# Sixty-four V gathers moved into the dense stage, eight expert groups per addition, and another DRAM order of the gate matrix

## The chip, the core and the metric

One NeuronCore of one Trainium2 chip runs the whole program in one launch. The metric is the device time in microseconds (us). A chip run lists the times of several executions, and their median counts. One further execution was recorded by the hardware profiler, and all rows below are of that one. Engines: PE does matmuls, DVE elementwise work, ACT activations and copies, POOL issues the indirect gathers, SP issues nearly all other DMAs.

## The reference, cut to what matters

A streaming-encoder layer (modulated norm, three mixers, output projection) is followed by a PEER expert layer. Each of 1024 tokens picks 16 experts in each of 8 heads out of 16384; expert e has a row `u_tab[e]` and a row `v_tab[e]` of 1024 float32.

```python
q = (ht @ w_q).reshape(ntok, 8, 2, 128)
s = einsum('thpd,pkd->thpk', q, sub_keys)            # two sets of 128 key scores
...                                                  # top 16 of the sums of both sets
gates = softmax(best)
act = gelu(einsum('td,thkd->thk', hb, u_tab[eb]))
out = einsum('thk,thkd->td', gb * act, v_tab[eb])
x = x + gt2 * out                                    # then a final RMS norm
```

## The kernel before

The 1024 tokens are eight tiles of 128. `front` computes the mixers for two tiles at a time (`("F", 0)` to `("F", 3)` in `PLAN`), and `product_keys` finds the experts of both. After that the expert layer is computed in two ways.

**Gathered tiles** (0, 1, 6, 7): a slot is one of a token's 128 experts. `u_slot` (L929) lets POOL gather one row of `u_tab` per token, 128 x 1024 float32, 512 KB, into a buffer `row`, and DVE multiplies it with the token and sums (L938). When all 128 slots of a tile are done, `v_slot` (L945) gathers rows of `v_tab` (L948), and DVE adds each, scaled, to `fin` (L953). Slots share 4 row buffers, 5 from the dense stage on (`RB`), so POOL runs at most that far ahead of DVE. `v_end` finishes a tile.

**Dense tiles** (2 to 5, 512 tokens): `gates` (L782) writes for each of these tokens a 128 x 128 matrix of gates, made by one-hot comparisons (DVE L793, ACT L797), a matmul (PE `gk`) and a copy to the tile `stg` (ACT L800, one buffer). A full `stg`, 16 tokens and 1 MB, goes to the DRAM tensor `gd` (L801); there are 32 of these writes. `dense` (L803) then walks all experts in 128 groups of 128: it loads the rows of U (`un`, L833), transposes them on PE (`T`, L851), splits them into a high part `uh` (ACT L852) and a low part `ul` (DVE L853), multiplies with the tokens (24 matmuls `A`), applies gelu (ACT `ag` L861), multiplies with the gates `gt` (DVE L868), splits into `w` (ACT L870, DVE L871) and multiplies with V rows (`vn`, split into `vh` and `vl`; 48 matmuls `V` per group). The V part is done for four groups at a time (`SG`), by quarters of the 1024 columns; each result is added to `acc` in SBUF (DVE L899). A gate tile `gt` holds eight groups, 2 MB (L836).

**Order.** Engines work in order; a scheduler has set each engine's order before the run. `PLAN` gives the order in the program, and a phase `("P", tu, tv)` of slots stands 3000 places lower in priority than where it is written (`PRI`), so slots fill what the front leaves. The slots of tile 0's V and tile 1's U stand beside fronts 2 and 3 and the gates; `("D",)` is the dense stage, and the slots written behind it run beside it.

Of the kernel before, what the change touches and what calls it, by code (L numbers as in the profile page):

```python
# [20 lines left out]
DM = 1024  # L21
# [9 lines left out]
AGB = 3  # L31
# [17 lines left out]
SG = 4  # L49
WB = 5  # L50
NQ = 4
UHB = 3
# [18 lines left out]
NS = HP * TOPK  # L71
NK = 128
# [15 lines left out]
def trunk(ctx, tc, x, c, w_mod, b_mod, g_mix, w_in, hgrn_lb_logits, s5_a_re, s5_a_im, s5_b_re, s5_b_im,  # L88
# [190 lines left out]
    gd = tc.dram_tile([ND // GT, 128, NK, GT], F32, name="gd")  # L279
# [505 lines left out]
    def gates(j, tT):  # L785

        for c in range(128 // GT):
# [13 lines left out]
            D.dma_start(out=gd[j * (128 // GT) + c], in_=stg)  # L801

    def dense():  # L803
# [13 lines left out]
        dpt, dpa, dpv = [pool(n, b, space=bass.MemoryType.PSUM) for n, b in (("dpt", 2), ("dpa", 2), ("dpv", 4))]  # L817
# [12 lines left out]
        for g in range(NK):  # L830
            rs_ = slice(g * 128, g * 128 + 128)
            un = dp.tile([128, DM], F32, name="un", bufs=UB)
# [10 lines left out]
            us = []  # L843
            for half in range(2):
                uh = dp.tile([128, 4, 128], F32R, name="uh", bufs=UHB)
                ul = dp.tile([128, 4, 128], F32R, name="ul", bufs=UHB)
                us.append((uh, ul))
                bk = dpt.tile([128, 4, 128], F32, name="T")
                for k in range(4):
                    kk = 4 * half + k  # L850
                    P_.transpose(bk[:, k], un[:, kk * 128:kk * 128 + 128], ident)  # L851
                S.copy(uh, bk)  # L852
                V.tensor_tensor(ul, bk, uh.bitcast(F32), OP.subtract)  # L853
            pA = dpa.tile([128, 512], F32, name="A")[:, 0:ND]
# [17 lines left out]
            ws.append(w)  # L872
            if len(ws) < SG:
                continue
            g0 = g + 1 - SG
            for qd in range(NQ):
                qs = slice(qd * QW, qd * QW + QW)
                vn = dv.tile([128, SG, QW], F32, name="vn", bufs=UB)
# [5 lines left out]
                for j0 in range(0, nt, 2):  # L884
# [440 lines left out]
```

## Time and profile before

| what | value |
|---|---|
| median of 3 runs | 3177.55 us (3175.67 to 3185.34) |
| the profiled execution, its own time | 3178.26 us |
| its span | 3176.5 us, 1.8 us less than its time |
| PE, DVE, POOL, ACT busy | 89%, 84%, 42%, 33% of the span |
| DMA moved | 896.72 MB, of it 536.94 MB by gathers |
| first and last matmul of the dense stage | 1582.1 and 3163.3 us |
| last gather issued | 3043.0 us |

The span has two halves. Up to 1582 us the fronts, the routing, the gate matrices and the slots of tiles 0 and 1 share the engines. From there to the end PE works through the 128 groups while DVE and POOL go through the slots of the other tiles. Busy shares are means over both.

### The profile page before, as it was taken

The numbers are of one execution on the slowest core, as the hardware profiler recorded it, in microseconds if no ns is written. First come the engines' busy times: TensorE is split into PE (matmuls) and PEld (weight loads), VectorE is DVE, ScalarE is ACT, GpSimd is POOL, SyncE is SP. The second block draws the span as 40 slices with busy tenths as digits, with TensorE's granted clock in tenths as the row PEclk, the third lists the DMA queues.
The fourth block names the chain that finished last, engine by engine and source line by source line (L and its number), as shares of the span: only waits on it lengthen the run. The fifth ranks groups of instructions, "written<-read, shape, count | busy, mean of one in ns | idle before, by whom it ended". The sixth has DMA issues, their size and how long they took to land.

```text
span 3176.5 us, 45427 instructions
## 1 busy us (share of the span) xinstructions
PE 2826.5 (89%) x16525; PEld 2416.8 (76%) x16525; DVE 2660.2 (84%) x5538; ACT 1037.4 (33%) x1958; POOL 1318.9 (42%) x1147
## 2 busy tenths in 40 slices
PE   5998975788788995689599999999999999999998
PEld 3765865466675874558589888899988888988887
DVE  6241798679987999889989989998999999898976
ACT  3212330132166660366622222222222222222223
POOL 0000156534444345542045545555555555354520
PEclk8998995889778995689599999999999999999999
DMA  4453587899779986898389999999999999899961
GB/s 152 117 167 122 163 308 240 306 330 317 229 239 334 312 307 234 269 346 289 133 309 346 354 327 340 349 345 340 355 334 352 346 347 345 311 326 317 352 224 60
DMA packets 419008, 896.72 MB, mean 282 GB/s; under 512 B 29416, under 2 KB 234848, under 8 KB 414688
## 3 DMA queue, kind: packets, MB, share of 16 engines
q0 software_dynamic: 147456, 536.94, 47.7%
q1 hardware_dynamic: 263680, 342.92, 32.3%
q10 hardware_dynamic: 7648, 13.96, 1.3%
q8 instruction: 130, 2.13, 0.3%
q14 instruction: 94, 0.77, 0.1%
HBM read 847.57 MB, written 46.14 MB: 281 GB/s over the span
## 4 chain that ended last, share of the span: by engine, by line
PE 43%; DVE 23%; DMA 13%; issue 11%; POOL 6%; ACT 4%; ACTq 0%; SPq 0%; POOLq 0%; DVEq 0%
PE V L139 13%; PE A L139 12%; PE bank L139 6%; DVE row L938 5%; DMA row<-in_peer_u_dram,eid 4%; DMA row<-in_peer_v_dram,eid 4%; PE wq L139 4%; POOL row L932 4%; PE bank L363 3%; DVE fin L953 3%; POOL row L948 3%; DVE oh L793 2%; PE T L851 2%; PE gk L139 1%; DMA gd<-stg 1%
## 5 line engine op out<-in xcount | busy, mean ns | idle before, releaser
L948 POOL DMA_INDIRECT row<-in_peer_v_dram,eid x512 | 636.0, 1242 | 662.5 <-DVE fin L953 365.9
L932 POOL DMA_INDIRECT row<-in_peer_u_dram,eid x512 | 643.7, 1257 | 619.3 <-DVE row L938 297.1
L139 PE MATMUL V<-vh,w 128*128 128x256 f32 x4096 | 767.7, 283 | 10.7 <-ACT w L870 4.4
L938 DVE SCALAR_TENSOR_TENSOR row<-row,h 128x1024 f32<-128x1024 f32 x512 | 619.9, 1219 | 84.7 <-DMA row<-in_peer_u_dram,eid 84.1
L953 DVE SCALAR_TENSOR_TENSOR fin<-row,wgt,fin 128x1024 f32<-128x1024 f32 x508 | 649.6, 1279 | 36.3 <-DMA row<-in_peer_v_dram,eid 33.9
L139 PEld LDWEIGHTS V<-vh,w 128*128 128x128 f32 x4096 | 643.2, 189 | 21.8 <-ACT w L870 6.9
L139 PE MATMUL V<-vl,w 128*128 128x256 f32 x2048 | 561.0, 281 | 2.6 <-DVE vl L883 2.6
L139 PE MATMUL A<-hh,ul 128*128 128x512 f32 x1024 | 406.7, 397 | 13.1 <-DVE ul L853 12.7
L139 PE MATMUL A<-hh,uh 128*128 128x512 f32 x1024 | 414.5, 405 | 0.4 <-ACT uh L852 0.3
L139 PE MATMUL A<-hl,uh 128*128 128x512 f32 x1024 | 403.5, 394 | 0.0
L139 PEld LDWEIGHTS V<-vl,w 128*128 128x128 f32 x2048 | 387.3, 189 | 7.8 <-DVE vl L883 4.5
L881 ACT CAST vh<-vn 128x1024 fp32r<-128x1024 f32 x128 | 134.7, 1052 | 460.0 <-PE V L139 427.0
L363 PE MATMUL bank<-hT,w 128*128 128x256 f32 x1152 | 269.8, 393 | 10.4 <-DMA w<-in_w_in_dram 6.9
L363 PEld LDWEIGHTS bank<-hT,w 128*128 128x128 f32 x1152 | 223.7, 198 | 45.1 <-DMA w<-in_w_in_dram 6.8
L139 PE MATMUL wq<-hT,w 128*128 128x256 f32 x1024 | 242.0, 389 | 7.4 <-DMA w<-in_peer_w_q_dram 6.0
L139 PEld LDWEIGHTS A<-hh,ul 128*128 128x128 f32 x1024 | 194.0, 189 | 53.8 <-DVE ul L853 19.9
L852 ACT CAST uh<-T 128x512 fp32r<-128x512 f32 x256 | 147.4, 587 | 264.5 <-PE T L851 261.2
L139 PEld LDWEIGHTS wq<-hT,w 128*128 128x128 f32 x1024 | 194.4, 196 | 35.1 <-DMA w<-in_peer_w_q_dram 4.7
L139 PEld LDWEIGHTS A<-hl,uh 128*128 128x128 f32 x1024 | 193.5, 189 | 36.1
L139 PEld LDWEIGHTS A<-hh,uh 128*128 128x128 f32 x1024 | 194.1, 190 | 34.7 <-ACT uh L852 1.3
L139 PE MATMUL gk<-oh 128*128 128x128 f32 x1024 | 173.6, 325 | 51.4 <-ACT oh L797 44.7
L139 PEld LDWEIGHTS gk<-oh 128*128 128x128 f32 x1024 | 160.5, 230 | 69.0 <-ACT oh L797 54.2
(423 smaller groups left out, 3977.5 us busy)
## 6 DMA issues: line engine op xcount, KB each, us to landing
vn<-in_peer_v_dram SPq DMA_DIRECT2D x128, 512.0 KB
un<-in_peer_u_dram SPq DMA_DIRECT2D x128, 512.0 KB
w<-in_w_in_dram SPq DMA_DIRECT2D x88, 512.0 KB
w<-in_peer_w_q_dram SPq DMA_DIRECT2D x64, 512.0 KB
gd<-stg SPq DMA_DIRECT2D x32, 1024.0 KB
gt<-gd SPq DMA_DIRECT2D x16, 2048.0 KB
w<-in_w_mod_dram SPq DMA_DIRECT2D x48, 512.0 KB
w<-in_w_out_dram SPq DMA_DIRECT2D x32, 512.0 KB
```

Source lines behind the costliest of these rows:

```text
L139: P_.matmul(o, l, r, start=st, stop=sp)
L363: P_.matmul(bk[:, i], w[:, k, i * 128:i * 128 + 128], hT[:, k0 + k], start=k0 + i + k == 0, stop=k0 + k == KT - 1, skip_group_check=True)
L793: V.tensor_tensor(oh, iof.unsqueeze(1).unsqueeze(1).to_broadcast([128, 2, 4, 128]), tT[:, 0:2, t4].unsqueeze(3).to_broadcast([128, 2, 4, 1 ...
L851: P_.transpose(bk[:, k], un[:, kk * 128:kk * 128 + 128], ident)
L852: S.copy(uh, bk)
L881: S.copy(vh, vn)
L932: G.indirect_dma_start(out=ur, out_offset=None, in_=u_tab, in_offset=bass.IndirectOffsetOnAxis(ap=o.eid[:, k:k + 1], axis=0))
L938: V.scalar_tensor_tensor(ur, ur, 1.0, o.h2, op0=OP.mult, op1=OP.mult, accum_out=o.act[:, k:k + 1])
L948: G.indirect_dma_start(out=vr, out_offset=None, in_=v_tab, in_offset=bass.IndirectOffsetOnAxis(ap=o.eid[:, k:k + 1], axis=0))
L953: V.scalar_tensor_tensor(o.fin, vr, o.wgt[:, k:k + 1], o.fin, op0=OP.mult, op1=OP.add)
```

## The change

- Tile 0's V slots 0 to 63 stay; slots 64 to 127 stand behind `("D",)` in `PLAN`, ahead of tile 1's V. One more buffer each of `eid` and `gate` keeps tile 0's data alive (`EB`).
- `SG` is 8: eight groups are summed in PSUM before one addition of 128 x 1024 to `acc`. V rows still come four groups at a time (`SB4`). `WB` is 8, so that one batch of `w` fills all its buffers.
- `T` is one PSUM buffer of 128 x 1024 where it was two of 128 x 512; `ul` is made by one DVE instruction per group; matmuls with `ul` come after the 16 with `uh`. `un` and `ag` have two buffers where they had three, `uh` and `ul` two of the whole width where they had three of half of it.
- `gd` lies in the order in which `gt` is read: a gate load reads 16 KB at one stretch per partition where it read runs of 512 bytes; a gate write writes 16 runs of 512 bytes per partition, 2 MB apart, where it wrote 8 KB at one stretch.
- The residual is added to `acc` four groups ahead of the end, in eight instructions.

```diff
-AGB = 3
+AGB = 2
...
-SG = 4
-WB = 5
+SG = 8
+SB4 = 4
+WB = 8
...
-UHB = 3
+UHB = 2
...
-PAD = 320
+PAD = 0
...
-EB = 3
-PLAN = [("F", 0), ("P", 0, None), ("F", 1), ("F", 2), ("G", 4), ("P", None, 0), ("P", 1, None), ("F", 3), ("D",), ("R",), ("P", None, 1), ("P", 6, None), ("P", 7, 6), ("P", None, 7), ("E",)]
+EB = 4
...
+PLAN = [("F", 0), ("P", 0, None), ("F", 1), ("F", 2), ("G", 4), ("P", None, 0, 0, 64), ("P", 1, None), ("F", 3), ("D",), ("R",), ("P", None, 0, 64, NS), ("P", None, 1), ("P", 6, None), ("P", 7, 6), ("P", None, 7), ("E",)]
...
-    gd = tc.dram_tile([ND // GT, 128, NK, GT], F32, name="gd")
+    gd = tc.dram_tile([NK // GA, 128, ND // GT, GA, GT], F32, name="gd")
...
-            D.dma_start(out=gd[j * (128 // GT) + c], in_=stg)
+            D.dma_start(out=gd[:, :, j * (128 // GT) + c].rearrange("o p a t -> p o a t"),
+                        in_=stg.rearrange("p (o a) t -> p o a t", a=GA))
...
-        dpt, dpa, dpv = [pool(n, b, space=bass.MemoryType.PSUM) for n, b in (("dpt", 2), ("dpa", 2), ("dpv", 4))]
+        dpt, dpa, dpv = [pool(n, b, space=bass.MemoryType.PSUM) for n, b in (("dpt", 1), ("dpa", 2), ("dpv", 2))]
...
-                D.dma_start(out=gt, in_=gd[:, :, g:g + GA].rearrange("c p a t -> p c a t"))
+                D.dma_start(out=gt, in_=gd[g // GA])
...
+            bk = dpt.tile([128, KT, 128], F32, name="T")
+            for k in range(KT):
+                P_.transpose(bk[:, k], un[:, k * 128:k * 128 + 128], ident)
             for half in range(2):
...
+                S.copy(uh[:, 4 * half:4 * half + 4], bk[:, 4 * half:4 * half + 4])
+            V.tensor_tensor(ul, bk, uh.bitcast(F32), OP.subtract)
             pA = dpa.tile([128, 512], F32, name="A")[:, 0:ND]
             for k in range(KT):
...
+                mm(pA, uh[:, k], hh[:, k], k == 0, False)
+                mm(pA, uh[:, k], hl[:, k], False, False)
+            for k in range(KT):
+                mm(pA, ul[:, k], hh[:, k], False, k == KT - 1)
...
+                pv = dpv.tile([128, nt, QW], F32, name="V")
+                for e0 in range(0, SG, SB4):
...
+                if g + 1 < NK:
+                    V.tensor_tensor(a, a, pv, OP.add)
+                    continue
...
-    def phase(tu, tv):
+    def phase(tu, tv, k0=0, k1=NS):
```

The built orders show it at three places. Names are the kernel's tiles; the changed kernel's line numbers are its own (its L938 and L954 are the gathers of U and V that were L932 and L948).

POOL, at the last routing of tiles 4 and 5 (the `cidx` copies), before and now:

```order
L932 DMA row<-in_peer_u_dram,eid 128x1024 x7
L716 COPY cid_6192<-cidx 128x4x8
L716 COPY cid_6192<-cidx 128x4x4
L716 COPY cid_6192<-cidx 128x4x2 x2
L716 COPY cid_6192<-cidx 128x4
L716 COPY cid_6192<-cidx 128x4x3
L932 DMA row<-in_peer_u_dram,eid 128x1024 x86
L948 DMA row<-in_peer_v_dram,eid 128x1024 x6
```

```order
L938 DMA row<-in_peer_u_dram,eid 128x1024 x7
L717 COPY cid_6192<-cidx 128x4x8
L717 COPY cid_6192<-cidx 128x4x4
L717 COPY cid_6192<-cidx 128x4x2 x2
L717 COPY cid_6192<-cidx 128x4
L717 COPY cid_6192<-cidx 128x4x3
L938 DMA row<-in_peer_u_dram,eid 128x1024 x4
L954 DMA row<-in_peer_v_dram,eid 128x1024 x7
L717 COPY cid_9626<-cidx 128x4x8
```

Of tile 1's U gathers 86 stood behind this routing, now 4; 63 V gathers of tile 0 that stood ahead of tile 1's U stand behind front 3. DVE's order follows: where the gates of the first two dense tiles are done, 276 slots have been consumed before and 285 now; up to the first `ul` of the dense stage 386 before and 323 now.

PE, in the dense stage between two groups, before and now:

```order
L851 MATMUL T<-ident,un 128x128 x4
L139 MATMUL V<-vh,w 128x256
L139 MATMUL V<-vl,w 128x256
L139 MATMUL V<-vh,w 128x256
L139 MATMUL V<-vl,w 128x256
L139 MATMUL V<-vh,w 128x256
L139 MATMUL A<-hh,ul 128x512
L139 MATMUL A<-hl,uh 128x512
L139 MATMUL A<-hh,uh 128x512
```

```order
L898 MATMUL V<-vh,w 128x256
L140 MATMUL A<-hh,ul 128x512 x8
L849 MATMUL T<-ident,un 128x128 x8
L898 MATMUL V<-vh,w 128x256
L898 MATMUL V<-vl,w 128x256
L140 MATMUL A<-hh,uh 128x512
L140 MATMUL A<-hl,uh 128x512
```

Before, V matmuls or matmuls of the other half of `T` stand between a transpose and what needs it all through the stage. Now each batch of eight groups begins with four that have at most two V matmuls behind their eight transposes (16 batches), then come groups with 8 to 26 V matmuls in between, then some 280 V matmuls almost without a break. Behind the last `A` 168 V matmuls stand before, 295 now.

DVE, around the last `w` of the dense stage, before and now:

```order
L871 TENSOR_TENSOR w<-ag,w 128x512
L868 TENSOR_TENSOR ag<-ag,gt 128x512
L871 TENSOR_TENSOR w<-ag,w 128x512
L898 TENSOR_TENSOR V<-V,gt_4569 128x512
L899 TENSOR_TENSOR acc<-acc,V 128x2x256
L898 TENSOR_TENSOR V<-V,gt_4569 128x512
L899 TENSOR_TENSOR acc<-acc,V 128x2x256
L883 TENSOR_TENSOR vl<-vn,vh 128x1024
```

```order
L867 TENSOR_TENSOR ag<-ag,gt 128x512
L959 SCALAR_TENSOR_TENSOR fin<-row,wgt,fin 128x1024
L870 TENSOR_TENSOR w<-ag,w 128x512
L959 SCALAR_TENSOR_TENSOR fin<-row,wgt,fin 128x1024
L891 TENSOR_TENSOR vl<-vn,vh 128x1024
L959 SCALAR_TENSOR_TENSOR fin<-row,wgt,fin 128x1024 x2
L909 TENSOR_TENSOR V<-V,gt_4569 128x512
L959 SCALAR_TENSOR_TENSOR fin<-row,wgt,fin 128x1024
L891 TENSOR_TENSOR vl<-vn,vh 128x1024
L910 TENSOR_TENSOR acc<-acc,V 128x2x256
L959 SCALAR_TENSOR_TENSOR fin<-row,wgt,fin 128x1024
```

Before, the last slot stands ahead of the last eight groups. Now slots go on to the end: 28 of the 1024 stand behind the last `w`. In both, some 44 slots stand among eight groups in the rest of the stage.

## Rows read from the trace of the kernel before

**Rows 1.** Busy time by stretch (windows): us, engines (instructions), granted clock, DMA.

```profile
core 0: us, PE busy (x) PEld busy (x) DVE busy (x) ACT busy (x) POOL busy (x), PEclk, DMA share, GB/s
640.00:1190.00 550.00, 477.17 (x2458) 394.72 (x2457) 494.42 (x1335) 263.64 (x579) 225.37 (x211) 0.89 0.86 295
1190.00:1335.00 145.00, 81.84 (x432) 73.66 (x430) 134.50 (x331) 18.35 (x26) 80.59 (x74) 0.64 0.76 253
1335.00:1577.00 242.00, 194.25 (x975) 162.58 (x975) 224.70 (x694) 173.71 (x409) 68.83 (x71) 0.82 0.71 256
1640.00:3040.00 1400.00, 1376.21 (x9088) 1242.50 (x9087) 1289.01 (x1711) 379.35 (x573) 765.09 (x615) 1.00 0.96 339
3045.00:3123.00 78.00, 76.96 (x538) 70.66 (x537) 52.80 (x87) 22.14 (x33) 0.00 (x0) 1.00 0.45 152
2400.00:2480.00 80.00, 80.00 (x554) 73.44 (x553) 75.01 (x102) 21.49 (x32) 45.61 (x37) 1.00 0.99 346
```

**Rows 2.** Groups by line, DVE, 640 to 1582 us.

```profile
L938 DVE SCALAR_TENSOR_TENSOR row<-row,h 128x1024 f32<-128x1024 f32 x149 | 179.7, 1216 | 25.2 <-DMA row<-in_peer_u_dram,eid 25.1
L953 DVE SCALAR_TENSOR_TENSOR fin<-row,wgt,fin 128x1024 f32<-128x1024 f32 x128 | 163.2, 1275 | 11.6 <-DMA row<-in_peer_v_dram,eid 11.2
```

**Rows 3.** Groups by line, DVE: first 1190 to 1335 us, then 1335 to 1577.

```profile
L938 DVE SCALAR_TENSOR_TENSOR row<-row,h 128x1024 f32<-128x1024 f32 x60 | 72.2, 1218 | 10.5 <-DMA row<-in_peer_u_dram,eid 10.3
L938 DVE SCALAR_TENSOR_TENSOR row<-row,h 128x1024 f32<-128x1024 f32 x44 | 53.2, 1218 | 8.1 <-DMA row<-in_peer_u_dram,eid 8.1
```

**Rows 4.** Groups by line, ACT, 1335 to 1577 us.

```profile
L797 ACT ACTIVATE oh<-oh,tT 128x128 f32<-128x128 f32 x256 | 81.2, 393 | 32.1 <-DVE oh L793 31.9
L800 ACT COPY stg<-gk 128x512 f32<-128x512 f32 x64 | 64.1, 1046 | 20.9 <-PE gk L139 12.1 <-DMA gd<-stg 8.6
```

**Rows 5.** Timeline, end of the front: SP, then PE.

```profile
1573.86 0.32 SPq L801 DMA_DIRECT2D gd<-stg  x1
1582.11 1.94 PE L851 MATMUL T<-ident,un 128*128 128x128 f32 x8 [9.37 <-issue]
```

**Rows 6.** Windows: one gate write (8 KB runs), one gate load (512-byte runs).

```profile
1553.50:1556.10 2.60, 2.33 (x13) 2.14 (x12) 2.60 (x16) 1.44 (x5) 0.00 (x0) 0.70 0.91 381
1580.50:1589.60 9.10, 7.49 (x23) 5.78 (x24) 5.64 (x8) 2.46 (x3) 0.00 (x0) 0.55 1.16 320
```

**Rows 7.** Groups by line, DVE, 1582 to 3170 us.

```profile
L853 DVE TENSOR_TENSOR ul<-T,uh 128x512 fp32r<-128x512 f32 x256 | 173.3, 685 | 21.0 <-ACT uh L852 20.8
L899 DVE TENSOR_TENSOR acc<-acc,V 128x512 f32<-128x512 f32 x248 | 167.8, 683 | 26.3 <-PE V L139 25.4
```

**Rows 8.** Timeline of SP over eight groups of experts.

```profile
2160.04 0.37 SPq L836 DMA_DIRECT2D gt<-gd  x1
2256.18 0.43 SPq L836 DMA_DIRECT2D gt<-gd  x1
```

**Rows 9.** Timeline of PE: second group of experts, nothing else to do.

```profile
1591.63 0.39 PE L139 MATMUL A<-hl,uh 128*128 128x512 f32 x1
1591.86 1.03 PE L851 MATMUL T<-ident,un 128*128 128x128 f32 x8
1593.19 0.50 PE L139 MATMUL A<-hh,uh 128*128 128x512 f32 x1 [0.29 <-ACT uh L852]
```

**Rows 10.** Waits of PE, 1582 to 3170 us: total, times, longest.

```profile
PE A L139 <- DVE ul L853: 12.7, 18, 1.7
```

**Rows 11.** Timeline of the end: DVE (three rows), and PE's last matmul.

```profile
3052.63 1.28 DVE L953 SCALAR_TENSOR_TENSOR fin<-row,wgt,fin 128x1024 f32<-128x1024 f32 x1 [0.67 <-DMA row<-in_peer_v_dram,eid]
3066.20 1.28 DVE L966 SCALAR_TENSOR_TENSOR fin<-fin,nw,row 128x1024 f32<-128x1024 f32 x1
3145.62 0.69 DVE L871 TENSOR_TENSOR w<-ag,w 128x512 fp32r<-128x512 f32 x1 [0.68 <-ACT w L870]
3163.33 0.28 PE L139 MATMUL V<-vh,w 128*128 128x256 f32 x1
```

More of the change, by code (lines that the diff above doesn't have):

```diff
@@ L831, in dense @@
             rs_ = slice(g * 128, g * 128 + 128)
[L832 removed]
+            un = dp.tile([128, DM], F32, name="un", bufs=2)
             D.dma_start(out=un, in_=u_tab[rs_])
@@ L872, in dense @@
             ws.append(w)
+            if g + 4 == NK:
+                for j in range(nt):
+                    V.tensor_tensor(acc[:, j], acc[:, j], bcast["gt2"], OP.mult)
+                    V.tensor_tensor(acc[:, j], acc[:, j], xq[:, j], OP.add)
             if len(ws) < SG:
@@ new lines, in dense @@
+                pv = dpv.tile([128, nt, QW], F32, name="V")
+                for e0 in range(0, SG, SB4):
+                    vn = dv.tile([128, SB4, QW], F32, name="vn", bufs=UB)
+                    r0 = (g0 + e0) * 128
+                    D.dma_start(out=vn, in_=v_tab[r0:r0 + SB4 * 128, qs].rearrange("(e p) d -> p e d", p=128))
+                    vh = dv.tile([128, SB4, QW], F32R, name="vh")
+                    S.copy(vh, vn)
+                    vl = dv.tile([128, SB4, QW], F32R, name="vl")
+                    V.tensor_tensor(vl, vn, vh.bitcast(F32), OP.subtract)
+                    for j in range(nt):
+                        js = slice(j * 128, j * 128 + 128)
+                        for e in range(SB4):
+                            w = ws[e0 + e]
+                            first, last = e0 + e == 0, e0 + e == SG - 1
+                            for i, (l, r) in enumerate(((w[:, 0, js], vh), (w[:, 1, js], vh), (w[:, 0, js], vl))):
+                                P_.matmul(pv[:, j], l, r[:, e], start=first and i == 0 and j % 2 == 0, stop=last and i == 2,
+                                          skip_group_check=True)
@@ new lines, in dense @@
+                a = acc[:, :, qs]
+                if g0 == 0:
+                    V.tensor_copy(a, pv)
+                    continue
+                if g + 1 < NK:
+                    V.tensor_tensor(a, a, pv, OP.add)
+                    continue
+                for j0 in range(0, nt, 2):
+                    a, p2 = acc[:, j0:j0 + 2, qs], pv[:, j0:j0 + 2]
+                    V.tensor_tensor(p2, p2, bcast["gt2"][:, qs].unsqueeze(1).to_broadcast([128, 2, QW]), OP.mult)
+                    V.tensor_tensor(a, a, p2, OP.add)
+                    for j in range(j0, j0 + 2):
+                        jk = dp.tile([128, ND], F32, name="ag", bufs=AGB)[:, 0:QW]
+                        S.activation(jk, acc[:, j, qs], AF.Square, accum_out=ss[:, j, qd:qd + 1])
+                    V.tensor_tensor(a, a, gfin[:, qs].unsqueeze(1).to_broadcast([128, 2, QW]), OP.mult)
@@ L940, in v_start @@
     def v_start(o):
-        o.wgt = pk_.tile([128, NS], F32, name="wgt")
+        o.wgt = pk_.tile([128, NS], F32, name="wgt", bufs=1)
         S.activation(o.wgt, o.act, AF.Gelu_apprx_tanh)
@@ L1010, in slots @@
             v = toks[tv]
-            v_start(v)
-        for k in range(NS):
+            if k0 == 0:
+                v_start(v)
+        for k in range(k0, k1):
             if o is not None:
@@ L1016, in slots @@
                 v_slot(v, k)
-        if v is not None:
+        if v is not None and k1 == NS:
             v_end(v)
```

53 lines of the change are left out of this document (6 added, 47 removed).

## The prediction, before the change was run

> **What bounds the kernel now.** I read the stretches first [rows 1]. From 1640 to 3040 us, the dense stage proper, PE is busy in 1376 of 1400 us at granted clock 1.00, the 2.4 GHz level, DVE in 1289 and DMA at a share of 0.96 with 339 GB/s: three resources run close to full at once. In the densest slice, 2400 to 2480, PE starts 554 matmuls in 80 us. A group has 80, so 92.4 us is about the least for eight groups, and SP's gate loads stand 96.1 us apart over eight groups [rows 8]. So PE is the bound, with some 4 us in 96 lost to what it waits for; DVE and DMA have little to give.
>
> Ahead of that, from 640 to 1577 us, DVE is the busiest: 494 of 550, 134.5 of 145 and 224.7 of 242 us [rows 1], and 343 of these 854 us are slots [rows 2]. PE waits there and its clock falls to 0.64 in the second stretch. The dense stage begins when the last gate write has left `stg`, whose memory it reuses: the write is issued at 1573.86 and the first transpose starts at 1582.11 [rows 5].
>
> I sum against the profiled execution, 3178.3 us, 1.8 over its span and 0.7 over the median of the runs. About 0.3%, some 10 us, is what a measurement can tell from no change.
>
> **The front.** By DVE's order 63 slots leave it, and what is left is shifted.
>
> *Up to 1190 us* nine more slots come in: 9 x 1.28 us [rows 2] is +12, and less if DVE's 56 idle us take some.
>
> *1190 to 1335 us.* The trace has 60 slots here [rows 3]; in the new order 38 stand from the end of the second tile's gates on, nearly all here. 22 x 1.22 is 27 us off a DVE that is busy in 134.5 of 145. I take -25, and keep -10 as an end, because the front's own chain from DVE to PE and back stays.
>
> *1335 to 1577 us.* The 44 slots here, 53 us [rows 3], go. DVE would fall from 225 to 171 us, and ACT, with 174 of 242 [rows 1], is the next bound: 145 of it are scalings and copies for 16 gate writes [rows 4], and `stg` has one buffer, so the first copy after a write waits until that has landed. Now that wait is 8.6 us in all [rows 4]. If each of 16 writes costs 2.6 us [rows 6], or 3.5 with short runs, and nothing covers it, ACT's 174 become 230, which leaves a gain of 12; if all is covered, the gain is 53. I take the middle, -32.
>
> Front: +12 - 25 - 32 = **-45**, with ends -80 and -10.
>
> **Gate matrix.** A gate write of 1 MB in long runs went at 381 GB/s with a DMA share of 0.91; a 2 MB gate load in 512-byte runs, other loads among it, at 320 GB/s with 1.16 [rows 6]. By rate the short runs cost 19% more DMA time, by rate per share 52%. For 33.6 MB that is 17 to 46 us; I take 30, off the dense stage and onto the front, where DMA is at 0.71 to 0.86 and can take it.
>
> The Trainium skill ("DMA: Bandwidth & Descriptors", Specifications) puts the least size for line rate at 512 bytes, so the layout would move nothing either way. The two windows do not agree, though others' packets are in them. By that rule the 30 us below would not come off, and the sum would be 3156.
>
> **The dense stage.**
>
> *DMA.* 63 gathers of 0.524 MB are 33 MB, 97 us at 339 GB/s. From 3045 to 3123 us the queues ran at 152 GB/s [rows 1]; up to 339 there is room for 43 us of it. With 30 from the gate loads, 24 us are left over: transfers would end near 3147 on the old clock, ahead of PE's 3163 [rows 11]. They fit, with nothing to spare.
>
> *DVE.* Slots add 63 x 1.28 = 81 us. Additions to `acc` took 248 x 0.683 = 168 and `ul` 173 us [rows 7]. An instruction twice as wide is not in the trace; its bounds are 1.22 us, that of the slot's multiply of 1024 elements from SBUF [rows 3], and 1.37, twice the 512. So 56 wide additions and 8 narrow ones make 74 to 82, 128 `ul` 156 to 175: 84 to 111 us less. DVE is not fuller than before, and per eight groups it has some 6 us less. I credit a third of PE's lost 3.7 us per eight groups to that: -20 in 16 batches (0 to -59).
>
> *PE.* The same matmuls stand in another order. Four groups in each batch have hardly anything between `T` and the `A` that needs it. The trace has one such place: 1.33 us from the first transpose to the next `A`, PE idle for 0.29 [rows 9]; the eight transposes need some 0.5 (92.4 / 8 less 24 at 0.23 and 48 at 0.115), so up to 0.8 is empty, and two V matmuls fill 0.23. Between 0.3 and 0.6 I take 0.4: 64 x 0.4 = +26. In turn PE's waits for `ul`, 12.7 us [rows 10], go, since 16 matmuls of 0.23 us now stand ahead of it: -13.
>
> *The end.* 127 more V matmuls stand behind the last `A`, so the last `w` is 15 us earlier for PE. Behind it stand 28 slots. With five row buffers 23 are still to come, 23 x 1.55 us at 339 GB/s, with six V loads 45 us. Then the last tile's finish: 14.9 us from the last slot's start to the end of the scaling [rows 11], and about 2 for the store. That is 62 behind the last `w`, where it was 31 (3145.6 to 3176.5): +31 - 15 = +16. I expect the last store to be tile 7's and no longer a dense tile's.
>
> Dense: -20 + 26 - 13 + 16 = **+9**, with ends -20 and +40. The sum is 3178.3 - 45 + 9 = **3142 us**; its own range, by the ends, is 3078 to 3208.
>
> **Rivals.**
>
> *The runs of four groups starve PE* (slower). With one `T` buffer, the next transposes wait until DVE has made `ul`; DVE works in order, and a slot ahead of `ul` can wait for its row, as slots now do for 37 us from 640 to 1582 us [rows 2]. Then `A` waits for `ul`, and nothing of V stands there to fill in. Against it: 3.7 us of matmuls stand ahead. From 0.55 us more per group of the 64 (35 us) the whole gain is gone; at 1.5 us the time is 3142 + 96 = 3238.
>
> *Gate writes hold ACT* (no change or slower). If each of the last 16 writes lands 3 us later than I allow, ACT stops in the copy behind it and DVE, PE and the dense stage's start with it: 16 x 3 = 48, 3190 us. For it: one buffer, and writes in the stretch that has just lost its other bound.
> The Trainium skill (same page, Latency and other measured facts) has copies at 164 GB/s with a 2 MiB row pitch where 512 KiB has 207; here the 16 runs of a partition lie 2 MB apart. No run here shows it yet.
>
> *All of it is gained* (faster). The front loses its 82 us, because the gates spread over it, and the lighter DVE brings PE near its floor in the dense stage: 3142 - 35 - 37 = 3070.
>
> That the slots do not move is excluded by the order; that they move and nothing shortens is the second rival.
>
> **Chances.** The forecast 0.53, starved PE 0.20, gate writes 0.12, all gained 0.15. Of the forecast's own range nine tenths lie below 3168. Faster by over 0.3%: 0.48 + 0.15 = 0.63. Within: 0.04 + 0.08 = 0.12. Slower: 0.25. The range leaves out most of the starved case and the far end of the best one: 3080 to 3205.
>
> **What would show it.** Right: the first dense transpose 30 to 60 us earlier, no slots between the third dense tile's gates, ACT's wait for gate writes up from 8.6 us in the last stretch; gate loads shorter; eight groups in 94 to 97 us; PE idle for 0.3 to 0.5 us ahead of `A` behind a bare `T`; the last store from tile 7. Wrong: a front that ends within 10 us of 1582, PE waits for `ul` of over 50 us, or eight groups in over 99 us.

## The result, and the profile after

The changed kernel took 3219.36 us in the median (3211.95 to 3226.33), the kernel before, run beside it, 3181.45: a ratio of 1.0119, 95% interval 1.0087 to 1.0151. I forecast 3142 in a range that ended at 3205. The profiled execution took 3226.33 us with a span of 3224.6. All sums below are of spans: 3224.6 - 3176.5 = +48. The medians differ by 38; the profiled execution of the changed kernel was the slowest of its four, so that some 7 us of the +48 are its own.

I cut each span in three: up to the first dense transpose (front), from there to the last `w` (dense), and what lies behind (end).

| kernel | front | dense | end | span |
|---|---|---|---|---|
| before | 1582.1 | 1563.5 | 30.9 | 3176.5 |
| changed | 1563.0 | 1583.0 | 78.7 | 3224.6 |
| difference | -19 | +19.5 | +48 | +48 |
| forecast | -45 | -22 | +31 | -36 |

(The forecast's dense stage is -20 + 26 - 13 and the 15 by which the last `w` comes earlier.)

The changed kernel's stretches, columns as in [rows 1]:

```profile
core 0: us, PE busy (x) PEld busy (x) DVE busy (x) ACT busy (x) POOL busy (x), PEclk, DMA share, GB/s
640.00:1190.00 550.00, 462.54 (x2342) 384.62 (x2340) 487.14 (x1366) 257.18 (x569) 236.59 (x218) 0.89 0.90 300
1190.00:1335.00 145.00, 101.92 (x576) 87.41 (x577) 124.50 (x319) 33.52 (x63) 53.08 (x50) 0.70 0.55 175
1335.00:1560.00 225.00, 183.98 (x956) 155.33 (x954) 156.83 (x566) 156.60 (x376) 4.65 (x24) 0.85 0.51 155
1640.00:3040.00 1400.00, 1359.03 (x8936) 1223.85 (x8935) 1212.94 (x1438) 367.75 (x566) 812.89 (x610) 1.00 0.94 338
3146.00:3211.00 65.00, 34.52 (x278) 34.15 (x278) 55.49 (x62) 15.59 (x41) 29.36 (x25) 0.78 0.82 281
```

The slots have left the stretches from 1190 to 1560 us: DMA's share there is 0.55 and 0.51, where it was 0.76 and 0.71 [rows 1], and DVE is busy in 157 of the last 225 us. Neither DVE nor ACT (157 of 225) is full there now, and yet the last 16 gate writes take 220 us from first to last, where they took 224. ACT by line, 1335 to 1560 us, answers to [rows 4]:

```profile
L798 ACT ACTIVATE oh<-oh,tT 128x128 f32<-128x128 f32 x232 | 74.1, 396 | 19.8 <-DVE oh L794 19.7
L801 ACT COPY stg<-gk 128x512 f32<-128x512 f32 x60 | 59.3, 1040 | 41.3 <-DMA gd<-stg 20.9 <-PE gk L140 20.4
```

The copy into `stg` waits 20.9 us for gate writes, where it waited 8.6. The gate loads did get shorter, as forecast: the last packet of one ends 10.0 us behind its issue in the mean over the dense stage, where it was 19.4.

Timeline of PE: the first dense transpose, which answers to [rows 5], and a place with a bare `T`, which answers to [rows 9].

```profile
1562.97 1.94 PE L849 MATMUL T<-ident,un 128*128 128x128 f32 x8 [10.58 <-DMA un<-in_peer_u_dram]
...
2178.71 1.77 PE L140 MATMUL A<-hh,ul 128*128 128x512 f32 x7
2180.32 1.03 PE L849 MATMUL T<-ident,un 128*128 128x128 f32 x8
2182.03 0.50 PE L140 MATMUL A<-hh,uh 128*128 128x512 f32 x1 [0.68 <-ACT uh L851]
```

From the transposes' start to the next `A` it is 1.71 us; eight transposes need 0.5 by the prediction's count. PE's waits from 1563 to 3170 us (total, times, longest):

```profile
PE A L140 <- ACT uh L851: 30.5, 58, 1.0
PE A L140 <- DVE ul L852: 2.1, 2, 1.2
```

The wait for `ul` has gone (12.7 us in [rows 10]); one for `uh` has come. DVE by line, 1563 to 3140 us, answers to [rows 7]:

```profile
L852 DVE TENSOR_TENSOR ul<-T,uh 128x1024 fp32r<-128x1024 f32 x128 | 156.1, 1220 | 15.5 <-ACT uh L851 15.2
L905 DVE TENSOR_TENSOR acc<-acc,V 128x1024 f32<-128x1024 f32 x56 | 68.2, 1218 | 32.5 <-PE V L898 32.3
```

An instruction twice as wide took 1.22 us, the lower of my two bounds. Timeline of DVE, the end:

```profile
3145.94 0.68 DVE L870 TENSOR_TENSOR w<-ag,w 128x512 fp32r<-128x512 f32 x1
...
3211.04 1.28 DVE L959 SCALAR_TENSOR_TENSOR fin<-row,wgt,fin 128x1024 f32<-128x1024 f32 x1 [1.23 <-DMA row<-in_peer_v_dram,eid]
3212.36 1.22 DVE L963 TENSOR_TENSOR fin<-fin,gt 128x1024 f32<-128x1024 f32 x1
...
3219.70 1.28 DVE L972 SCALAR_TENSOR_TENSOR fin<-fin,nw,row 128x1024 f32<-128x1024 f32 x1
```

The last `w` is where it was [rows 11]. 65 us later the last slot is computed, and tile 7's finish follows.

### The profile page after: what moved, and what is told of

Same layout as the page of the kernel before. It is cut to its first block, busy times and chain, and to the rows that moved or that the text cites. A ratio compares the mean times of both kernels' runs of the same rounds, so it can differ in the third digit from the quotient of the medians.

```text
span 3224.6 us, 45205 instructions
## 1 busy us (share of the span) xinstructions
PE 2831.6 (88%) x16525; PEld 2420.1 (75%) x16525; DVE 2585.1 (80%) x5214; ACT 1026.5 (32%) x1956; POOL 1375.2 (43%) x1147
## 4 chain that ended last, share of the span: by engine, by line
PE 47%; DMA 16%; DVE 15%; issue 11%; POOL 6%; ACT 5%; ACTq 0%; POOLq 0%; SPq 0%; DVEq 0%
PE V L898 13%; PE A L140 12%; PE bank L140 7%; DMA row<-in_peer_v_dram,eid 6%; PE wq L140 5%; PE bank L364 5%; POOL row L954 4%; DMA gd<-stg 3%; DVE row L944 3%; PE gk L140 3%; DMA row<-in_peer_u_dram,eid 3%; DVE fin L959 2%; POOL row L938 2%; PE T L849 2%; DMA w<-in_w_in_dram 1%
## 5 line engine op out<-in xcount | busy, mean ns | idle before, releaser
L938 POOL DMA_INDIRECT row<-in_peer_u_dram,eid x512 | 661.8, 1293 | 626.1 <-DVE row L944 294.4
L954 POOL DMA_INDIRECT row<-in_peer_v_dram,eid x512 | 677.2, 1323 | 578.6 <-DVE fin L959 288.7
L898 PE MATMUL V<-vh,w 128*128 128x256 f32 x4096 | 748.6, 282 | 18.9 <-ACT vh L889 6.1
L898 PEld LDWEIGHTS V<-vh,w 128*128 128x128 f32 x4096 | 634.4, 190 | 32.5 <-ACT vh L889 9.2
L898 PE MATMUL V<-vl,w 128*128 128x256 f32 x2048 | 569.9, 280 | 0.6 <-DVE vl L891 0.6
L140 PE MATMUL A<-hh,uh 128*128 128x512 f32 x1024 | 411.1, 401 | 32.9 <-ACT uh L851 30.5
L364 PE MATMUL bank<-hT,w 128*128 128x256 f32 x1152 | 269.9, 392 | 13.0 <-DMA w<-in_w_in_dram 10.6
L860 ACT ACTIVATE ag<-A 128x512 f32<-128x512 f32 x128 | 76.6, 598 | 621.6 <-PE A L140 602.4
L140 PE MATMUL A<-hh,ul 128*128 128x512 f32 x1024 | 258.4, 394 | 2.2 <-DVE ul L852 2.1
L364 PEld LDWEIGHTS bank<-hT,w 128*128 128x128 f32 x1152 | 222.6, 197 | 47.9 <-DMA w<-in_w_in_dram 9.5
L794 DVE TENSOR_TENSOR oh<-iof,tT 128x1024 f32<-128x1024 f32 x128 | 154.6, 1215 | 83.4 <-PE gk L140 69.0
L140 PEld LDWEIGHTS A<-hh,ul 128*128 128x128 f32 x1024 | 186.0, 189 | 38.9 <-DVE ul L852 3.2
```

The costliest lines, as they stand in the source:

```text
L140: P_.matmul(o, l, r, start=st, stop=sp)
L364: P_.matmul(bk[:, i], w[:, k, i * 128:i * 128 + 128], hT[:, k0 + k], start=k0 + i + k == 0, stop=k0 + k == KT - 1, skip_group_check=True)
L794: V.tensor_tensor(oh, iof.unsqueeze(1).unsqueeze(1).to_broadcast([128, 2, 4, 128]), tT[:, 0:2, t4].unsqueeze(3).to_broadcast([128, 2, 4, 1 ...
L898: P_.matmul(pv[:, j], l, r[:, e], start=first and i == 0 and j % 2 == 0, stop=last and i == 2, skip_group_check=True)
L938: G.indirect_dma_start(out=ur, out_offset=None, in_=u_tab, in_offset=bass.IndirectOffsetOnAxis(ap=o.eid[:, k:k + 1], axis=0))
L954: G.indirect_dma_start(out=vr, out_offset=None, in_=v_tab, in_offset=bass.IndirectOffsetOnAxis(ap=o.eid[:, k:k + 1], axis=0))
```

## The experiments

The table has the three parts of each run's span. "New order" is the new order of `gd`, "moved" the number of V slots moved, and SG the number of groups per addition. The changed kernel's front was run in three kernels, and ended at 1563.0, 1559.3 and 1550.5 us: some 6 us either way is scatter of one profile. The dense stages of e4_layout_only and e7_pitch, which differ in unused rows of DRAM alone, lie 6.5 us apart.

| run | new order | moved | SG | front | dense | end | ratio to before (95%) |
|---|---|---|---|---|---|---|---|
| e1_no_move | yes | 0 | 8 | 1603.7 | 1565.1 | 48.0 | 1.0107 (1.0072 to 1.0142) |
| e3_move_only | no | 64 | 4 | 1537.4 | 1573.3 | 100.0 | 1.0111 (1.0069 to 1.0153) |
| e4_layout_only | yes | 0 | 4 | 1600.0 | 1577.3 | 30.8 | 1.0101 (1.0052 to 1.0150) |
| e6_split96 | yes | 32 | 8 | 1587.6 | 1569.7 | 46.5 | 1.0100 (1.007 to 1.013) |
| e2_old_layout | no | 64 | 8 | 1524.0 | 1603.9 | 80.3 | 1.0128 (1.0097 to 1.0159) |
| e7_pitch | yes, padded | 0 | 4 | 1602.7 | 1583.8 | 31.6 | 1.0115 (1.0087 to 1.0142) |
| e11_load4k | yes, 4 KB loads | 0 | 4 | 1605.1 | 1555.5 | 30.6 | 1.0075 (1.0046 to 1.0104) |
| e10_move32 | no | 32 | 4 | 1577.3 | 1562.5 | 33.8 | 1.0006 (0.9988 to 1.0025) |
| e13_load_alone | loads only | 0 | 4 | 1586.5 | 1555.9 | 30.5 | 0.9969 (0.9950 to 0.9988) |
| e9_stg2 | no | 0 | 4 | 1816.7 | 1571.1 | 31.9 | 1.0766 (1.0719 to 1.0814) |
| e12_stg2_layout4k | yes, 4 KB loads | 0 | 4 | 1830.1 | 1562.9 | 30.6 | 1.0781 (1.0734 to 1.0829) |
| e14_after_load4k | yes, 4 KB loads | 64 | 8 | 1559.3 | 1583.7 | 75.2 | 1.0100 (1.0076 to 1.0124) |
| e15_drop28 | yes | 64 | 8 | 1550.5 | 1585.0 | 47.9 | 1.0015 (0.9998 to 1.0033) |
| e17_hybrid | half, 4 KB loads | 0 | 4 | 1591.2 | 1552.4 | 30.5 | 0.9996 (0.9981 to 1.0012) |
| e16_hybrid_move32 | half, 4 KB loads | 32 | 4 | 1580.4 | 1557.2 | 32.6 | 0.9997 (0.9983 to 1.0012) |

By spans, the change can be built up in three steps: the new order of `gd` alone costs 32 us (e4_layout_only), the eight-group form on top of it 9 (e1_no_move), and the move on top of both 8 (the changed kernel). But the parts do not simply add: the move alone costs 34 us (e3_move_only), and the change without the new order still costs 32 (e2_old_layout).

### The parts one by one

The changed kernel without the move (it keeps `SG = 8` and the new order):

```diff
-PLAN = [..., ("P", None, 0, 0, 64), ("P", 1, None), ("F", 3), ("D",), ("R",), ("P", None, 0, 64, NS), ...]
+PLAN = [..., ("P", None, 0), ("P", 1, None), ("F", 3), ("D",), ("R",), ...]
```

> The changed kernel with all 128 V slots of tile 0 back ahead of the dense stage; everything else as changed. Theory M (the move costs more than it gives, because the 28 slots behind the last w share DVE with the last batch's epilogue): no slot stands behind the last w, so the end comes some 45 to 50 us behind the last w where the changed kernel has 79; the front ends near 1582 us again (19 later than the changed one); total 3185 to 3195, under the changed kernel's 3219. Rival T (the new order of A, T and V in the dense stage makes all of the loss): eight groups still take 100 us, the total stays at 3205 to 3220. Rival L (gate writes in 512-byte runs hold the front): first dense transpose 10 or more us behind 1582.

The end is 48.0 us without one slot behind the last `w`, as theory M has it, but the span is 3216.8, where only the rivals T and L had it: the move is not most of the loss. The front ends at 1603.7 us, so the move brings it 41 us forward (to 1563.0), and what kept the changed front from -45 was something else. In return the move lengthens the dense stage by 18 us (1565.1 to 1583.0) and the end by 31: the moved slots do not fit.

The kernel before with the move alone:

```diff
-EB = 3
+EB = 4
-PLAN = [..., ("P", None, 0), ...]
+PLAN = [..., ("P", None, 0, 0, 64), ..., ("D",), ("R",), ("P", None, 0, 64, NS), ...]
```

> The kernel before with the move alone (64 V slots of tile 0 behind the dense stage's start, one more eid and gate buffer, one wgt buffer): old dense stage, old gate layout. In its order 42 slots stand behind the last w. Theory M: the front gains about the 19 us that it gained in the changed kernel, the end comes 80 to 100 us behind the last w, total 3210 to 3230. Rival L: without the short-run gate writes the front gains 30 us or more, first dense transpose before 1552. Rival T: total at or under 3180, since the dense stage is the old one.

Its first dense transpose, in PE's timeline:

```profile
1537.42 1.94 PE L852 MATMUL T<-ident,un 128*128 128x128 f32 x8 [8.81 <-DMA un<-in_peer_u_dram]
```

That is 44.7 us before 1582.1 [rows 5], the -45 of the forecast, and rival L's sign; the end (100.0) and the span (3210.8) are theory M's. For 42 slots stand behind the last `w`; DVE by line from 3111 us:

```profile
L954 DVE SCALAR_TENSOR_TENSOR fin<-row,wgt,fin 128x1024 f32<-128x1024 f32 x42 | 53.8, 1282 | 15.6 <-DMA row<-in_peer_v_dram,eid 14.8
```

They take 54 us, and DVE is idle for 15.6 more ahead of them. The end grows by 69 us and the dense stage by 10, more than the front gave.

The kernel before with the new order of `gd` alone (the write is the change's too):

```diff
-    gd = tc.dram_tile([ND // GT, 128, NK, GT], F32, name="gd")
+    gd = tc.dram_tile([NK // GA, 128, ND // GT, GA, GT], F32, name="gd")
-                D.dma_start(out=gt, in_=gd[:, :, g:g + GA].rearrange("c p a t -> p c a t"))
+                D.dma_start(out=gt, in_=gd[g // GA])
```

> The kernel before with the gate matrix's new order in DRAM alone. Theories M and T: within 10 us of before (3171 to 3191), first dense transpose 0 to 8 us later, DMA share in the dense stage a little lower (0.94 to 0.95 against 0.96). Rival L: ACT's wait for gate writes doubles from 27 us and the total is over 3191.

The front is 18 us later and the dense stage 14 us longer, though slots and matmuls stand in nearly the same order. ACT's waits for gate writes over the whole span, first before, then here:

```profile
ACT stg L800 <- DMA gd<-stg: 27.1, 16, 4.2
```

```profile
ACT stg L800 <- DMA gd<-stg: 64.6, 21, 6.1
```

The new order alone costs 1%, and rival L held. In this form it gives the dense stage nothing.

The changed kernel with 32 slots moved instead of 64:

```diff
-("P", None, 0, 0, 64) ... ("P", None, 0, 64, NS)
+("P", None, 0, 0, 96) ... ("P", None, 0, 96, NS)
```

> The changed kernel with the split at slot 96 in place of 64: 32 slots move, and in its order none stands behind the last w. Theory M: the end is 45 to 50 us behind the last w as without the move, the front ends 5 to 12 us earlier than 1582, total 3175 to 3192, the best of the changed family. Rival T: 3200 or more, since eight groups still take 100 us.

No slot stands behind the last `w`, and the end is 46.5. But the front gives 16 us of the 41, and the span is 3203.8, as rival T had it.

The changed kernel with the old order of `gd` (the reverse of the edit to `gd` above):

```diff
-    gd = tc.dram_tile([NK // GA, 128, ND // GT, GA, GT], F32, name="gd")
+    gd = tc.dram_tile([ND // GT, 128, NK, GT], F32, name="gd")
```

> The change with the gate matrix in the old order; all else as changed. Theory (the layout costs on the front and gives the dense stage nothing): first dense transpose at 1537 to 1548 us as in the run with the move alone (changed kernel: 1563), eight groups in 99.2 to 100 us (changed: 100.2), the part behind the last w 75 to 85 us as in the changed kernel, span 3195 to 3205. Rival (the layout pays in the dense stage when eight groups are summed, since DMA is fuller there): first transpose the same 1540, but eight groups over 100.5 and the span 3220 or more.

The front came even earlier, 1524.0. But the dense stage took 1603.9 us, 102.0 for eight groups and in three of its batches 109 to 112: the rival's number for eight groups held, by another cause, and its span (3220) did not. One such batch by stretch (columns as in [rows 1]), and SP's timeline and ACT's in it:

```profile
1797.90:1906.80 108.90, 99.97 (x640) 90.25 (x640) 90.04 (x83) 25.91 (x41) 66.78 (x47) 0.95 0.92 321
```

```profile
1797.28 14.41 SPq L834 DMA_DIRECT2D un<-in_peer_u_dram  x1
1811.74 21.72 SPq L886 DMA_DIRECT2D vn<-in_peer_v_dram  x5
```

```profile
1825.98 1.04 ACT L888 CAST vh<-vn 128x1024 fp32r<-128x1024 f32 x1 [16.11 <-DMA vn<-in_peer_v_dram]
```

SP stands 14.4 us on a `un` load, for which only two buffers are left, and five `vn` loads are issued behind it, so ACT stands 16.1 us before its next V rows. Over the dense stage ACT's waits for `vn` are 155 us here and 21 in the changed kernel. What reaches PE of that is less, from 1640 to 3040 us, here and in the changed kernel:

```profile
PE V L897 <- ACT vh L888: 21.5, 10, 6.0
```

```profile
PE V L898 <- ACT vh L889: 4.9, 6, 3.1
```

In the three long batches the granted clock was 0.95 to 0.97 besides, where most others have 1.00 (2.4 GHz). No run gives this form a third buffer of `un`, so that two buffers are the reason is argued and not shown.

### What the new order costs, and where

First the distance between the runs of a write, padded to 2.03 MB:

```diff
-    gd = tc.dram_tile([NK // GA, 128, ND // GT, GA, GT], F32, name="gd")
+    gd = tc.dram_tile([NK // GA, 130, ND // GT, GA, GT], F32, name="gd")
```

> The kernel before with the new gate order, in which each run of eight experts' rows is followed by two unused rows, so that a partition's 16 runs of a gate write lie 2.03 MB apart and no longer at 2 MB exactly. Theory of the pitch (runs 2 MB apart share some resource of the memory): the packets of an undisturbed gate write last 2.6 us again where they lasted 3.2, ACT's waits for gate writes fall from 65 us towards the 27 of the kernel before, and the first dense transpose comes at 1582 to 1588 us where it came at 1600. Rival (512-byte runs cost it, whatever their pitch): 3.2 us, some 60 us of waits, 1597 to 1603.

The rival held. The front ends at 1602.7 us, ACT's waits are these, and the last five writes, with hardly anything else on the queues, land 4.1 us after their issue, as with the exact 2 MB (3.4 in the kernel before); their packets last 3.2 us in both and 2.6 before.

```profile
ACT stg L800 <- DMA gd<-stg: 55.1, 17, 6.8
```

So the distance is not what makes a write longer; what is left of the edit to the writes is the shorter runs. The Trainium skill ("DMA: Bandwidth & Descriptors", Latency and other measured facts) has copies slower at a 2 MiB row pitch than at 512 KiB. That pitch is from one partition's row to the next, here it lies between the runs of one partition, and no part of such a loss shows here.

Then the size of the pieces that a gate load is cut into, in the kernel before with the new order:

```diff
-                D.dma_start(out=gt, in_=gd[g // GA])
+                for c4 in range(0, ND // GT, 8):
+                    D.dma_start(out=gt[:, c4:c4 + 8], in_=gd[g // GA, :, c4:c4 + 8])
```

> The kernel before with the new gate order, but each gate load in four transfers of eight chunks, 4 KB at one stretch per partition where it was 16 KB. In the run with the new gate order alone the gathers fell to 75 GB/s from 2 to 8 us behind a gate load's issue, where they had 109 to 249 GB/s in the kernel before. Theory (pieces of 16 KB hold the gathers' pieces of 4 KB back): gathers at over 120 GB/s in those 6 us, DVE's waits for rows from 1640 to 3040 us back from 79 to some 50, eight groups back from 99.5 to 98.8 us, span some 10 us shorter than 3208. Rival (2 MB of gate rows take the same share of DMA however they are cut): gathers under 100 GB/s there, 99.4 us or more.

The DMA queues from 2 to 8 us behind the issue of one gate load, picked close to the mean (packets, MB, share of 16 engines; q0 are the gathers): before, then 16 KB pieces, then 4 KB.

```profile
q1 hardware_dynamic: 1851, 0.95, 61.0%
q0 software_dynamic: 263, 0.99, 43.4%
```

```profile
q1 hardware_dynamic: 129, 1.97, 80.4%
q0 software_dynamic: 121, 0.45, 18.9%
```

```profile
q1 hardware_dynamic: 303, 1.13, 58.9%
q0 software_dynamic: 240, 0.87, 38.0%
```

The gathers move 0.99, 0.45 and 0.87 MB in these 6 us. Over the 13 or 14 loads of the stage the mean is 165, 75 and 146 GB/s (70 in the changed kernel). DVE's waits for rows, 1640 to 3040 us, with 16 KB and with 4 KB:

```profile
DVE row L939 <- DMA row<-in_peer_u_dram,eid: 43.9, 38, 5.3
DVE fin L954 <- DMA row<-in_peer_v_dram,eid: 35.1, 25, 4.8
```

```profile
DVE fin L955 <- DMA row<-in_peer_v_dram,eid: 36.7, 36, 2.4
DVE row L940 <- DMA row<-in_peer_u_dram,eid: 28.1, 32, 2.7
```

They fell from 79 to 65 us, not to the 50 that I expected; the kernel before has 44. Eight groups came down from 99.3 to 97.9 us (before: 98.4; mean of the 15 distances between the last `w` of batches). So 16 KB pieces hold the gathers back, and with 4 KB the new order does pay in the dense stage: 8 us less than before. That gain does not come through the rows, for which DVE waits longer than before; where it comes from stays open. The front still loses 23.

Reading alone, with the old writes, so that the loads take other tokens' gates:

```diff
+    gdw = gd.rearrange("(c p a t) -> c p a t", c=ND // GT, p=128, t=GT)
+    gdr = gd.rearrange("(o p c a t) -> o p c a t", o=NK // GA, p=128, a=GA, t=GT)
```

> Reading side alone: gate writes as in the kernel before (8 KB at one stretch), gate loads from the same memory as if it lay in the new order, in four transfers with 4 KB at one stretch. The loads take gates of other tokens and experts, so that the output is not the reference's; all instructions and sizes are the same. Theory (the writes alone delay the front, the cut of the loads alone moves the dense stage): first dense transpose at 1580 to 1585 us as before, dense stage to the last w 8 us shorter than before's 1563.5, eight groups in 97.9 us, span 3165 to 3172. Rival (the 8 us in the run with 4 KB pieces came from its later start and order and not from the loads): first transpose 1582, dense 1563, span 3175.

Both halves are apart now: the front ends at 1586.5, within its scatter of 1582.1, and the dense stage is 7.6 us shorter. The write side costs the front 18 to 23 us against 1582.1 in the three runs with new writes and no other change of the front, 13 to 19 against this run. The read side gives 8, in the next pair of runs too (1571.1 and 1562.9). Nothing but this run was faster than the kernel before, and it is a measurement, no version.

Whether ACT's stop at `stg` is what delays the front: two buffers of `stg`, first in the old order, then in the new one.

```diff
-OB = 2
+OB = 1
-WPB = 3
+WPB = 2
-            stg = gp.tile([128, NK, GT], F32, name="stg", bufs=1)
+            stg = gp.tile([128, NK, GT], F32, name="stg", bufs=2)
```

> The kernel before with two buffers for stg in place of one; to make room, one buffer for the one-hot tiles (of 2) and two for the front's weights (of 3). It is the base for the next run, not a candidate: 71 more slots stand ahead of the first dense group in its order, so its front is longer, by up to 71 x 1.25 = 89 us; first dense transpose at 1620 to 1670. ACT's waits for gate writes, 27.1 us with one buffer, under 8.

> The run before this one with the new gate order, loads in 4 KB pieces. Theory (the new order delays the front only because ACT stands still until a write has left the single stg): with two buffers ACT's waits for gate writes stay under 15 us and the first dense transpose lies within 6 us of the run before this one. Rival (the short runs delay the front by taking DMA time from gathers and loads): it comes 15 to 22 us later, as it did with one buffer, while ACT's waits are small.

The base was slower than I thought, 1816.7 us: that is 235 us, of which the slots that moved in explain 89 at most. The rest must be the two buffers taken away, which were not tried apart. ACT has no wait for gate writes left in either run. Yet the new order comes later, by timelines of PE:

```profile
1816.74 1.94 PE L851 MATMUL T<-ident,un 128*128 128x128 f32 x8 [16.13 <-issue]
```

```profile
1830.09 1.94 PE L853 MATMUL T<-ident,un 128*128 128x128 f32 x8 [22.17 <-issue]
```

The second comes 13.4 us later, between my two expectations. 7 of it are in the issue of the last gate write (1802 and 1809 us), the rest in its landing. So ACT's wait is at most a part of the cause; the longer writes delay the front without it too. How the 18 us divide stays open, given the scatter.

Only the first 16 writes in the new order, the others in the old one, in a second tensor:

```diff
+            if jc < NC:
+                D.dma_start(out=gn[:, :, jc].rearrange("o p a t -> p o a t"),
+                            in_=stg.rearrange("p (o a) t -> p o a t", a=GA))
+            else:
+                D.dma_start(out=gd[jc - NC], in_=stg)
```

> The kernel before with the gates of the first two dense tiles (the first 16 writes) in the new order, loaded in 4 KB pieces, and those of the last two in the old order; no slots moved. In the run with the new order for all, the 16th write was issued 5 us later than before (1195 and 1190 us) and the last one 17 us later (1591 and 1574). Theory (only the last 16 writes hold the front up, the loads gain in proportion): first dense transpose 3 to 7 us later than 1582.1, dense stage up to the last w 3 to 5 us shorter than 1563.5, span 3173 to 3180, no difference that can be told. Rival (half of the short runs, half of the delay): first transpose at 1591 or later, span 3182.

The front's 1591.2 is at the rival's edge, 5 to 9 us over the two runs with old writes. It does not speak for the rival: the 17th write, where the short runs have ended, is issued 2 us later than before (1352 and 1350), and the rest comes among writes in the old order, while ACT waits for writes in 9.9 us of the whole span, less than the 27.1 before. The dense stage gains 11, more than in proportion. The time is that of the kernel before. The same with 32 slots moved (the `PLAN` of 96):

> The run before this one with 32 V slots moved into the dense stage. With 32 moved and the old gate order the first dense transpose came at 1577.3, the last w at 3139.8 and the span was 3173.6. Theory (both parts add): first transpose at 1578 to 1584, dense stage to the last w 1556 to 1560, end 31 to 34, span 3166 to 3174, at best 0.3% under the kernel before. Rival (the moved slots take the DMA time that the larger loads give back, and slots end up behind the last w): span 3176 or more.

The three parts came out as expected in the profile, but the median over 12 runs shows no gain. It is no better kernel. Nor is the smaller move by itself (`PLAN` of 96 in the kernel before, `EB = 4`):

> The kernel before with 32 of the V slots moved into the dense stage where the change moves 64; four groups per addition and the old gate order stay. Theory (slots go at some 44 per eight groups whatever stands there, and those left over come out at the end; the front gives 0.7 us per moved slot): first dense transpose at 1560 us, one slot behind the last w so that the end grows from 31 us to at most 55, span 3170 to 3185. If the end stays at 31 to 40 us it is faster than the kernel before: 3155 to 3168. Rival (each moved slot costs the dense stage as much as it gives the front): 3176 whatever the end does.

Only one slot stands behind the last `w` and the end is 33.8, but the front gave 5 us where I expected 22, and the time is that of the rival. The place of the slots says why. These 32 empty the last stretch: among the last 16 gate writes stand no slots where 40 stood, and these writes take 13 us less, while 9 slots more come in ahead of the 16th write. The next 32, in the run with the move alone, leave the stretch between the 16th and the 17th write (31 slots, 65 before), which gets 36 us shorter than before, and the front ends 40 us earlier than here. In the changed kernel the two halves bring 16 and 25 us.

### What the changed dense stage lost

The changed kernel with 4 KB loads (the diff of the loads above):

> The changed kernel with each gate load in four transfers, 4 KB at one stretch in place of 16 KB. Theory (16 KB pieces hold the gathers back for some 6 us behind each load): eight groups from 100.2 to some 99 us, DVE's waits for rows from 1640 to 3040 us from 87 to under 70, the last w 15 us earlier than 3145.9, the span 10 to 16 us shorter: 3208 to 3215. Rival (with eight groups summed PE's own gaps set the pace, not the gathers): eight groups at 100, span 3222.

The rival held: the gathers' rate behind a load rose from 70 to 130 GB/s, and the dense stage stayed at 1583.7 us. In this form of the stage the gathers do not set the pace. ACT's waits for `vn` rose to 98 us, but PE's for `vh` are 7.0 us, so they do not set it either.

The changed kernel without the 28 slots behind the last `w`:

```diff
-        for k in range(k0, k1):
+        for k in range(k0, k1 - 28 if tv == 7 else k1):
```

> The changed kernel without the last 28 V slots of tile 7, those that stand behind the last w; the order up to there is the same. These slots are not computed, so that the output lacks them. Theory (the slots behind the last w are the end's excess): the last w stays at 3146 us within 4, the end behind it falls from 78.7 to 46 to 50 us, as in the run without the move, span 3192 to 3197. Rival (the 295 V matmuls and the additions of the eight-group batch need that time anyway): 65 us or more, span over 3210.

DVE's timeline, from the last `w` to the last scaling, which is now a dense tile's:

```profile
3135.50 0.68 DVE L870 TENSOR_TENSOR w<-ag,w 128x512 fp32r<-128x512 f32 x1
...
3175.20 1.42 DVE L929 TENSOR_SCALAR acc<-acc,st 128x1024 f32<-128x1024 f32 x2
```

The end is 47.9 us where it was 78.7, as the theory has it. The last `w` came ten us earlier, and the span with it: the first dense transpose stood at 1550.5 us, and as the edit stands far behind it, I take that for scatter of the front. So of the +48 of the end 31 are the 28 slots, 1.1 us each, and 17 the batch of eight groups.

## Why the prediction was wrong, step by step

**The front, -45.** The total was right for the move: -44.7 in the old order of `gd`. Its parts were not, and their errors cancelled, which is luck. By the issues of the gate writes in that run it is +3 up to the 16th write (forecast +12), -36 from there to the 17th (-25) and -11 behind (-32). In the last stretch 40 slots, 49 us of DVE, left and gave 11 to 13 us. The gates there run through DVE, ACT, PE and `stg` in turn; that this chain and not DVE's load sets the pace is argued, not shown.

**"30 us off the dense stage and onto the front, where DMA can take it": this step failed,** with the wrong sign at both ends. I read DMA's share of 0.71 to 0.86 as room, and let the longer writes into the sum only by a bound of the last stretch. The dense stage starts behind the last write, and the new order alone made the front 18 us longer; the changed front is 19 us early where the move had brought 41 to 45. And I counted packet time as if saved time were gained time. In the sum the 30 us stood as room for the moved slots, worth 14 us there (3156 - 3142). The packets of the gate loads did get shorter, but the long pieces halved the gathers' rate behind each load, and the dense stage grew by 14 us in the same run. Cut to 4 KB, 8 of the 30 came.

The Trainium skill ("DMA: Bandwidth & Descriptors", Specifications) has 512 bytes as the least size for line rate, by which nothing should have changed. The trace does not agree for these writes: an undisturbed write took 4.1 us in runs of 512 bytes and 3.4 in runs of 8 KB.

The rival "gate writes hold ACT" named the place, though not the dense stage. The runs with two buffers show that ACT's wait is not the whole of it. If each of 32 writes came through with its 0.7 us in full, that would be 22 us, an estimate; how the 18 us of front come about was not taken apart.

**DVE lighter, -20: failed.** The relief came as worked out: `ul` and the wide additions take 156.1 + 68.2 us, for 173.3 + 167.8 [rows 7], and DVE is busy in 1213 of 1400 us, not 1289 [rows 1]. PE gained nothing: eight groups took 100.7 us where I expected 94 to 97 (over 99 was my sign of being wrong), and 99.7 without the move, where the four-group form in the same order of `gd` has 99.3. That form is 12 us slower up to the last `w` (1577.3 and 1565.1), but only by the first eight groups (87 and 70 us): the eight-group form leaves V matmuls for later, the 15 us that I counted, and pays 17 of end.

**Bare `T`, +26: mis-sized.** The mechanism was right, the price low. The time between the starts of an `A` and of the matmul ahead of it, over what that matmul needs, grew by 25 us behind V matmuls and by 14 behind `T`: +39. At [rows 9]'s place PE was idle for 0.29 us, at the one shown above for 0.68. **Waits for `ul`, -13:** right, 12.7 to 2.1. The rival of starved PE, by way of `ul`, is refuted; what `A` waits for is ACT's `uh`, 30.5 us.

**"They fit, with nothing to spare": this step failed too.** I put the moved slots' cost to the dense stage at nothing, by adding up DMA's time. In the changed form they lengthen the stage by 18 us and the end by 31, against 41 off the front; how the 18 arise was not taken apart. DMA's share is 0.94 in the changed stage and was 0.96 [rows 1], and some 44 slots go with eight groups in either; the moved ones fill the last batch, which had none, and come out behind it.

**The end, +31: mis-sized, +48.** I counted one chain, the slots' at DMA's pace, and put the last batch's own work at nothing. Both run on DVE, which is busy in 55.5 of the 65 us behind the last `w`:

```profile
L959 DVE SCALAR_TENSOR_TENSOR fin<-row,wgt,fin 128x1024 f32<-128x1024 f32 x29 | 37.1, 1279 | 7.6 <-DMA row<-in_peer_v_dram,eid 7.4
L891 DVE TENSOR_TENSOR vl<-vn,vh 128x1024 fp32r<-128x1024 f32 x5 | 6.2, 1231 | 1.9 <-ACT vh L889 1.9
L909 DVE TENSOR_TENSOR V<-V,gt 128x512 f32<-128x512 f32 x8 | 5.5, 691 | 0.1
L914 DVE TENSOR_TENSOR acc<-acc,un 128x512 f32<-128x512 f32 x8 | 5.4, 680 | 0.0
L910 DVE TENSOR_TENSOR acc<-acc,V 128x512 f32<-128x512 f32 x8 | 5.4, 677 | 0.0
```

37 us of slots and some 23 of the last batch add up; DMA's rows are waited for in 7.4 us only. That tile 7 would finish last was right.

## What to carry to other kernels

Work that is moved into a stage without free room comes out behind it: count what is left when the stage is over, and add up the chains that share an engine there. Take work out of a stretch only where its engine sets the pace: 34 slots gave 36 us in one stretch of the front, 40 gave 13 in the next. Unused DMA share in a stretch is no room for a transfer that the next stage waits for. A change of layout has two sides: test writing and reading by themselves, and look at what the larger pieces do to the other queue, not only at their own time.

## What the runs showed of the hardware

- 2 MB loads in 16 KB pieces on one queue cut the gathers of 4 KB pieces on another to 75 GB/s for 6 us (e4_layout_only); in 4 KB (e11_load4k) or 512-byte pieces (before) the same bytes left them 146 and 165. The load's own time is no measure of that: its last packet came 10.6, 11.7 and 19.4 us behind the issue.
- A write of 1 MB to DRAM with hardly anything else on the queues landed 4.1 us after its issue in runs of 512 bytes, 2 MB or 2.03 MB apart, and 3.4 us in runs of 8 KB.
- An instruction of 128x1024 on DVE took 1.22 us with PSUM as a source (`ul`, `acc`), as with SBUF alone [rows 3]; two of half the size took 1.37.
